# A two-layer hybrid block on one Trainium2 core: the MLP rewritten in two stages over DRAM, with its up-projection in pairs of output tiles by Strassen's seven block products

## The chip, the cores and the metric

The kernel runs on one core of one Trainium2 chip. The metric is the device time of one execution in microseconds (us). The time before is 2850.98 us, the median of three runs (2849.66 to 2864.86). The profile is that of one further execution; its own time stands in the table below, beside its span.

## The reference

Two layers (`DEPTH = 2`) over 1024 tokens of width 1024 (`D`), all in fp32. In each layer a modulated norm, a mixer (differential attention, latent attention and a state-space branch), a residual, a second modulated norm, an MLP of width 4096 (`FF`) and a residual. The part that matters here:

```python
def _sq_relu_mlp(h, w_up, w_down):
    return jnp.square(jax.nn.relu(h @ w_up)) @ w_down

for l in range(DEPTH):
    mod = (cond @ w_ada[l] + b_ada[l])[:, None, :]
    sh_m, sc_m, g_m, sh_f, sc_f, g_f = jnp.split(mod, 6, axis=-1)
    ...
    h = _rmsnorm(x, norm_g[l, 2]) * (1.0 + sc_f) + sh_f
    y = _sq_relu_mlp(h, w_up[l], w_down[l])
    x = x + g_f * _rmsnorm(y, norm_g[l, 3])
```

## The kernel before

Every fp32 operand of a matmul is split in two: a rounded high part, made by a copy on ScalarE (ACT), and the remainder, made by a subtraction on VectorE (DVE). A product of two fp32 blocks is then three matmuls (`mm3`, L192 to L194): high by high, high by low, low by high. Each matmul is 128 x 128 weights against 512 columns, and its sum stands in a PSUM bank (`bank_b` of 512 columns, `bank_s` of 1024, `bank_t` for small things).

The hidden state `hT` (high `hh`, low `hl`) lies transposed in SBUF, 8 blocks `k` of 128 channels by 1024 tokens. `mlp` walks over the 32 tiles `f` of 128 hidden features in groups, `GROUPS = [3]*2 + [2]*11 + [4]`. For each `f`, `load_up` brings 512 KB of `w_up` (L207) and splits it (L210 on ACT, L211 on DVE); `up` makes the two halves of 512 tokens, 24 matmuls each; `Relu` and `Square` on ACT (L221, L222), a product on GpSimd (POOL, L223) and a subtraction on DVE (L224) leave the activated tile `r` split in SBUF; `load_down` brings `w_down` for that `f` and splits it (L229, L232, L233). At the end of a group the eight token tiles each take their down-projection, 6 matmuls for each `f`, into `bank_s`, and the result is added to `y` in SBUF (a copy L273 for the first group, a DVE addition L275 after that). Activations never leave SBUF. Eight slots of the array `split` (`self.R`) hold the weights and the tiles `r`; eight more hold `hT`.

Three streams of other work are threaded through. `late` finishes the residual, norm and transposition of the last token tiles (L1156, L1157, L494, L495, L503 to L506) between the two token halves of the first group. `bg` is the matrix-vector product for the next layer's modulation (`mod_stream`): 56 chunks, each with a 512 KB load (L419), 8 DVE instructions of 128 x 128 (L434) and small matmuls (L445). It is advanced by `next(bg)`, two chunks a call, once for each `f`, and exists in layer 0 alone. `finish` runs the residual and norm of a token tile in the last group.

A scheduler with a timeline of its own orders the instructions of each engine at build time; on the chip each engine then takes them in that order. SP issues all DMAs.

## Time and profile before

| | |
|---|---|
| time, median of 3 runs | 2850.98 us (2849.66 to 2864.86) |
| the profiled execution | 2852.23 us, its span 2850.5 us |
| mean granted TensorE clock | 0.962 |
| instructions | 34146 |
| PE (matmul) busy | 2705.3 us, 95% of the span |
| DVE busy | 1574.3 us, 55% |
| ACT busy | 941.4 us, 33% |
| POOL busy | 595.0 us, 21% |
| DMA moved | 239.66 MB, 84 GB/s over the span |

Busy times are sums over the span and say nothing of where an engine waits. The MLP of layer 0 stands from about 731 to 1451 us, that of layer 1 from about 2141 to 2840 us; the mixers stand before them. PE is TensorE's matmuls, PEld its weight loads, which run beside the matmuls. A matmul's recorded time (0.39 us) is longer than the distance from one to the next (0.23 us), since they are pipelined.

### The profile page before, as it was taken

Reading aid. Unit: us, or ns where it says so; the run is one execution under the profiler, and the core shown is the slowest. Engines: PE = TensorE matmul, PEld = TensorE weight load, DVE = VectorE, ACT = ScalarE, POOL = GpSimd, SP = SyncE. Lnnn points to the kernel's source line nnn. Section 1 sums busy time; section 2 is a strip of 40 time slices with the busy share of each in tenths; the row PEclk is TensorE's granted clock in tenths of the full one; section 3 lists DMA queues with packets and bytes.
Section 4 is the critical chain, followed back from the end, with each engine's and each line's share of the span. In section 5 each row is a group of like instructions: output and inputs, shape, how many; then the busy total and the mean of one; then the engine's idle time right before and its main releaser. Section 6 shows DMA issues by size and latency. Waiting matters only on the chain.

```text
span 2850.5 us, 34146 instructions
## 1 busy us (share of the span) xinstructions
PE 2705.3 (95%) x12914; PEld 2128.9 (75%) x12914; DVE 1574.3 (55%) x2860; ACT 941.4 (33%) x1841; POOL 595.0 (21%) x516
## 2 busy tenths in 40 slices
PE   5799998998899999999979999989989999999998
PEld 4677776676777787887868776667768888888886
DVE  7767677544735557566483667664453344343334
ACT  5243444544421212212243434354443222121122
POOL 1341244201200111111160114241021111110113
PEclk9899999999999999999989999789989999999999
DMA  6441312313322323233340221141142121111112
GB/s 223 115 136 50 93 60 87 109 59 107 115 82 89 96 74 119 80 98 88 101 154 10 64 87 63 54 129 58 49 133 74 45 74 48 41 59 33 57 45 104
DMA packets 258697, 239.66 MB, mean 84 GB/s; under 512 B 22818, under 2 KB 226788, under 8 KB 258532
## 3 DMA queue, kind: packets, MB, share of 16 engines
q1 hardware_dynamic: 258532, 237.47, 26.9%
q8 instruction: 102, 1.67, 0.2%
q14 instruction: 63, 0.52, 0.1%
HBM read 204.56 MB, written 32.87 MB: 83 GB/s over the span
## 4 chain that ended last, share of the span: by engine, by line
PE 74%; DVE 5%; DMA 4%; issue 3%; ACT 2%; POOL 1%; POOLq 0%; SPq 0%; DVEq 0%; ACTq 0%
PE bank_b L192 12%; PE bank_b L194 12%; PE bank_b L193 12%; PE bank_s L192 8%; PE bank_s L193 8%; PE bank_s L194 8%; PE bank_a L737 3%; PE bank_s L790 2%; PE bank_t L750 2%; PE bank_b L1083 1%; DMA arena_f<-in_w_ada 1%; PE bank_s L503 1%; PE bank_a L766 1%; DVE arena_f L434 1%; PE bank_b L884 1%
## 5 line engine op out<-in xcount | busy, mean ns | idle before, releaser
L192 PE MATMUL bank_b<-split 128*128 128x512 f32 (+2 forms) x1952 | 771.5, 396 | 10.1 <-ACT split L505 5.4
L193 PE MATMUL bank_b<-split 128*128 128x512 f32 (+2 forms) x1952 | 755.7, 387 | 4.3 <-DVE split L514 3.6
L194 PE MATMUL bank_b<-split 128*128 128x512 f32 (+2 forms) x1952 | 754.5, 387 | 2.5 <-DVE split L211 2.0
L192 PE MATMUL bank_s<-split 128*128 128x512 f32 (+2 forms) x1152 | 453.5, 396 | 8.3 <-ACT split L1310 3.5
L193 PE MATMUL bank_s<-split 128*128 128x512 f32 (+2 forms) x1152 | 450.7, 391 | 3.3 <-DVE split L1311 1.6
L194 PE MATMUL bank_s<-split 128*128 128x512 f32 (+2 forms) x1152 | 445.5, 390 | 0.7 <-DVE split L224 0.7
L192 PEld LDWEIGHTS bank_b<-split 128*128 128x128 f32 x1952 | 375.7, 193 | 89.2 <-issue 7.6
L193 PEld LDWEIGHTS bank_b<-split 128*128 128x128 f32 x1952 | 375.8, 193 | 74.4 <-issue 4.3
L194 PEld LDWEIGHTS bank_b<-split 128*128 128x128 f32 x1952 | 374.1, 192 | 75.5 <-issue 2.6
L275 DVE TENSOR_TENSOR arena_f<-arena_f,bank_s 128x1024 f32<-128x1024 f32 x208 | 253.1, 1219 | 314.3 <-PE bank_s L194 314.2
L223 POOL TENSOR_TENSOR arena_f<-arena_f 128x512 f32<-128x512 f32 x128 | 164.4, 1284 | 996.0 <-ACT split L222 945.9
L192 PEld LDWEIGHTS bank_s<-split 128*128 128x128 f32 (+1 forms) x1152 | 218.4, 190 | 60.5 <-ACT arena_f L725 4.6
L193 PEld LDWEIGHTS bank_s<-split 128*128 128x128 f32 (+1 forms) x1152 | 219.2, 190 | 50.4 <-issue 2.9
L194 PEld LDWEIGHTS bank_s<-split 128*128 128x128 f32 (+1 forms) x1152 | 219.0, 190 | 45.5 <-DVE split L224 1.4
L221 ACT ACTIVATE arena_f<-bank_b 128x512 f32<-128x512 f32 x128 | 76.1, 595 | 467.2 <-PE bank_b L194 467.1
L725 ACT ACTIVATE arena_f<-bank_s,nm 128x128 f32<-128x128 f32 (+3 forms) x192 | 141.8, 740 | 185.1 <-DVE nm L724 157.2
L724 DVE TENSOR_REDUCE nm<-bank_s 128x1 f32<-128x128 f32 (+3 forms) x192 | 141.7, 751 | 109.3 <-PE bank_s L939 64.7
L232 ACT CAST split<-arena_f 128x1024 fp32r<-128x1024 f32 x64 | 67.3, 1052 | 386.6 <-PE bank_s L194 287.8
L224 DVE TENSOR_TENSOR split<-arena_f,split 128x512 fp32r<-128x512 f32 x128 | 88.3, 690 | 181.1 <-POOL arena_f L223 181.1
L434 DVE SCALAR_TENSOR_TENSOR arena_f<-arena_f,cond 128x128 f32<-128x128 f32 x448 | 154.6, 379 | 60.8 <-DMA arena_f<-in_w_ada 31.0
L233 DVE TENSOR_TENSOR split<-arena_f,split 128x1024 fp32r<-128x1024 f32 x64 | 81.3, 1271 | 84.0 <-ACT split L232 83.9
L790 PE MATMUL bank_s<-split 32*128 32x512 f32 (+3 forms) x576 | 114.7, 376 | 13.2 <-ACT arena_f L725 10.7
(261 smaller groups left out, 3137.2 us busy)
## 6 DMA issues: line engine op xcount, KB each, us to landing
arena_f<-in_w_ada SPq DMA_DIRECT2D x80, 512.0 KB
arena_f<-in_w_down SPq DMA_DIRECT2D x64, 512.0 KB
arena_f<-in_w_up SPq DMA_DIRECT2D x64, 512.0 KB
arena_f<-d_x SPq DMA_DIRECT2D x36, 512.0 KB
d_x<-arena_f SPq DMA_DIRECT2D x24, 512.0 KB
arena_f<-in_w_in SPq DMA_DIRECT2D x20, 512.0 KB
arena_f<-in_w_ada SPq DMA_DIRECT2D x8, 1024.0 KB
arena_f<-in_x SPq DMA_DIRECT2D x16, 512.0 KB
```

Source lines behind the costliest of these rows:

```text
L192: mm(out, wh, xh, start=start, stop=False)
L193: mm(out, wh, xl, start=False, stop=False)
L194: mm(out, wl, xh, start=False, stop=stop)
L223: nc.gpsimd.tensor_mul(t, t, t)
L224: nc.vector.tensor_sub(r[:, 1, sl], t, f32(r[:, 0, sl]))
L233: nc.vector.tensor_sub(wd[:, 1], st, f32(wd[:, 0]))
L275: nc.vector.tensor_add(y[t], y[t], ps)
L434: nc.vector.scalar_tensor_tensor(acc, in0=w[:, k], scalar=self.cond[:, k:k + 1], in1=acc, op0=ALU.mult, op1=ALU.add)
L724: nc.vector.tensor_reduce(nm, S[:, 0:n], axis=AX.X, op=ALU.max, negate=True)
L725: nc.scalar.activation(p[:, 0:n], S[:, 0:n], AF.Exp, bias=nm, accum_out=ls)
L737: nc.tensor.matmul(bk[jj * 64:jj * 64 + 64, 128 * half:256], v[:, 2 * c + jj], e[:, 256:384] if half else e[:, jj * 256:jj * 256 + 256], s ...
L790: nc.tensor.matmul(S[mp][:, c0:c1], Q[rw, a, tok], K[rw, b, c0:c1], start=a == b, stop=a == 1 and c1 < n)
```

## The change

`mlp` becomes two functions. `mlp_up` makes all 32 activated tiles and stores them in a DRAM array `d_r` (4 stores of 256 KB for each pair of tiles). `mlp_down` loads them again, 512 KB for each `f` beside the 512 KB of `w_down`, splits both (ACT and DVE), and makes the down-projection in `GROUPS = [2] + [4]*6 + [2, 4]`.

In `mlp_up` the tiles f = 0 to 3 are made as before, the first two around `late`. The other 28 are made in 14 pairs. A pair's block of the product is 2 x 2 (two feature tiles by two token halves) with the 1024 channels in two halves, and is made of seven products of 12 matmuls each (Winograd's form of Strassen's scheme): 84 matmuls where the plain way has 96. For this four sums of blocks of `hT`, `T[0]` to `T[3]`, are formed once in each layer by `form` (48 instructions of 128 x 512 on DVE, 16 on POOL, and a copy for each on ACT), each pair's weights are combined by four POOL instructions and split in seven `cut`s into a ring of four places, and the seven products are combined by DVE additions that read one operand from PSUM. `bg` is advanced 15 times in `mlp_up` and then once for each `f` in `mlp_down`. In `mlp_down` sixteen slots are taken in turn; for the last two groups their list is sorted, so that these begin again with slot 0.

Around the end of the first stage in layer 1 (tiles f = 0, 1 done, `hT` complete), VectorE's rows before the change, from the last part of `hT` (L506) on, are the subtractions for `r`, `w_up` and `w_down`:

```order
L506 TENSOR_TENSOR split<-bank_s,split 128x8x128
L224 TENSOR_TENSOR split<-arena_f,split 128x512
L233 TENSOR_TENSOR split<-arena_f,split 128x1024
L224 TENSOR_TENSOR split<-arena_f,split 128x512
L211 TENSOR_TENSOR split<-arena_f,split 128x1024
L224 TENSOR_TENSOR split<-arena_f,split 128x512 x2
```

And now, from the last part of `hT` (now L607) to the subtraction for the weights of f = 2 (the first `L200` of 128x1024):

```order
L607 TENSOR_TENSOR split<-bank_s,split 128x8x128 x2
L248 TENSOR_TENSOR arena_f<-split 128x512 x4
L249 TENSOR_TENSOR arena_f<-split 128x512 x4
L250 TENSOR_TENSOR arena_f<-arena_f 128x512 x4
L200 TENSOR_TENSOR split<-arena_f,split 128x512
L248 TENSOR_TENSOR arena_f<-split 128x512
L200 TENSOR_TENSOR split<-arena_f,split 128x512
...
L249 TENSOR_TENSOR arena_f<-split 128x512
L200 TENSOR_TENSOR split<-arena_f,split 128x512
L248 TENSOR_TENSOR arena_f<-split 128x512
L200 TENSOR_TENSOR split<-arena_f,split 128x1024
```

The subtraction that f = 2 needs is now the 22nd VectorE instruction behind `hT` (the 20th in layer 0), behind instructions of `form`. At the same place POOL had its additions of the norm (L495) and the products of `up` (L223):

```order
L495 TENSOR_TENSOR arena_f<-arena_f 128x1024 x7
L223 TENSOR_TENSOR arena_f<-arena_f 128x512
L495 TENSOR_TENSOR arena_f<-arena_f 128x1024
L223 TENSOR_TENSOR arena_f<-arena_f 128x512 x63
L524 TENSOR_TENSOR arena_f<-arena_f 128x1024 x8
```

And has now the whole of form 2, all of it with two inputs from SBUF:

```order
L596 TENSOR_TENSOR arena_f<-arena_f 128x1024 x8
L248 TENSOR_TENSOR arena_f<-split 128x512 x4
L249 TENSOR_TENSOR arena_f<-split 128x512 x3
L250 TENSOR_TENSOR arena_f<-arena_f 128x512 x3
L200 TENSOR_TENSOR split<-arena_f,split 128x512 x3
L249 TENSOR_TENSOR arena_f<-split 128x512
L250 TENSOR_TENSOR arena_f<-arena_f 128x512
L200 TENSOR_TENSOR split<-arena_f,split 128x512
```

So 16 POOL instructions of 128x512 stand ready together with VectorE's. The third place is VectorE in layer 0 before the first down-projections. Before, the work of `bg` (L434) stood in short runs between the subtractions and the additions to `y` (L275):

```order
L434 SCALAR_TENSOR_TENSOR arena_f<-arena_f,cond 128x128 x7
L211 TENSOR_TENSOR split<-arena_f,split 128x1024
L434 SCALAR_TENSOR_TENSOR arena_f<-arena_f,cond 128x128
L224 TENSOR_TENSOR split<-arena_f,split 128x512
L434 SCALAR_TENSOR_TENSOR arena_f<-arena_f,cond 128x128 x3
L224 TENSOR_TENSOR split<-arena_f,split 128x512
```

Now, from the last addition of the last pair (L333) on, long runs of it (now L535) stand ahead of the subtractions (L200) that the second group of the down-projection needs:

```order
L333 TENSOR_TENSOR arena_f<-arena_f,bank_b 128x512
L200 TENSOR_TENSOR split<-arena_f,split 128x1024
...
L535 SCALAR_TENSOR_TENSOR arena_f<-arena_f,cond 128x128 x28
L554 TENSOR_TENSOR arena_f<-bank_t,arena_f 1x128 x2
L535 SCALAR_TENSOR_TENSOR arena_f<-arena_f,cond 128x128 x33
L200 TENSOR_TENSOR split<-arena_f,split 128x1024
L535 SCALAR_TENSOR_TENSOR arena_f<-arena_f,cond 128x128
L200 TENSOR_TENSOR split<-arena_f,split 128x1024
L535 SCALAR_TENSOR_TENSOR arena_f<-arena_f,cond 128x128
L200 TENSOR_TENSOR split<-arena_f,split 128x1024 x3
```

Between L333 and the last of these subtractions stand 74 instructions L535. The mixer of layer 0 keeps its order; in the mixer of layer 1 the scheduler has put the same instructions partly in another order.

The diff, cut to its core:

```diff
-GROUPS = [3] * 2 + [2] * 11 + [4]
+GROUPS = [2] + [4] * 6 + [2, 4]
...
+    def split(self, src, hi, lo, eng=None):
+        self.nc.scalar.copy(hi, src)
+        (eng or self.nc.vector).tensor_sub(lo, src, f32(hi))
...
+    def mlp_up(self, l, hT, bg, late):
...
+        def store(f, hf, t):
+            r = F.get(512) if t.tensor is not self.F.t.tensor else t
+            nc.scalar.activation(r, t, AF.Relu)
+            nc.scalar.activation(r, r, AF.Square)
+            dma(self.d_r[l][f, :, half[hf]], r)
+            F.put(r)
...
+        ws = [load_plain(f) for f in range(2)]
+        for hf in range(2):
+            for f in range(2):
+                up(f, ws[f], hf)
+            self.drain(late)
+        T = [self.slot(2 * n, 2, 4, 512) for n in range(4)]
+        def form(n, a, b, eng):
+            for k in range(4):
+                c, d = F.get(512), F.get(512)
+                eng.tensor_sub(c, f32(a[0][:, k]), f32(b[0][:, k]))
+                eng.tensor_sub(d, f32(a[1][:, k]), f32(b[1][:, k]))
+                eng.tensor_add(c, c, d)
+                self.split(c, T[n][:, 0, k], T[n][:, 1, k], eng)
+                F.put(c, d)
...
+        form(0, B(0, 1), B(0, 0), nc.vector)
+        form(1, B(1, 1), part(0), nc.vector)
+        for f in range(2, 4):
+            w = load_plain(f)
+            for hf in range(2):
+                up(f, w, hf)
+        form(2, B(1, 1), B(0, 1), nc.gpsimd)
+        form(3, B(1, 0), part(1), nc.vector)
+        next(bg, None)
...
+        def forms(i):
+            st = F.get(KD, 2 * P)
+            dma(st, w_up[:, :, i * 2 * P:(i + 1) * 2 * P])
...
+            yield cut(a11)
+            yield cut(a12)
+            s1, s2 = F.get(4, P), F.get(4, P)
+            nc.gpsimd.tensor_add(s1, a21, a22)
+            nc.gpsimd.tensor_sub(s2, s1, a11)
+            yield cut(s2)
+            nc.gpsimd.tensor_sub(a21, a11, a21)
+            yield cut(a21)
+            yield cut(s1)
+            nc.gpsimd.tensor_sub(s2, a12, s2)
+            yield cut(s2)
+            F.put(s1, s2)
+            yield cut(a22)
+            F.put(st)
+        queue = [next(parts) for _ in range(3)]
...
+            for k in range(4):
+                self.mm3(ps, w[0][:, k], w[1][:, k], b[0][:, k], b[1][:, k], k == 0, k == 3)
...
+        for i in range(2, N):
+            f = 2 * i
+            ps, p1 = product(B(0, 0)), F.get(512)
+            nc.scalar.copy(p1, ps)
+            ps, c = product(B(1, 0)), F.get(512)
+            add(c, p1, ps)
+            store(f, 0, c)
...
+            ps = product(part(3))
+            add(u3, u3, ps)
+            store(f + 1, 0, u3)
+            next(bg, None)
...
+    def mlp_down(self, l, y, bg, finish):
+        free = [2, 3, 4, 5, 0, 1, 6, 7, *range(8, 16)]
...
+            if f0 + GROUPS[-1] >= FF // P:
+                free.sort()
...
+            for f in fs:
+                rw.append((load(self.d_r[l][f]), load(w_dn[f * P:(f + 1) * P, :])))
                 next(bg, None)
...
+        self.d_r = [dt(f"d_r{l}", [FF // P, P, T]) for l in range(DEPTH)]
...
+            with self.phase(t=1, b=3):
+                self.mlp_up(l, hT, bg, late)
             with self.phase(t=2, b=2):
-                self.mlp(l, hT, y, bg, late, finish)
+                self.mlp_down(l, y, bg, finish)
```

More of the change, by code (lines that the diff above doesn't have):

```diff
@@ new lines, in mlp_up @@
+        part = lambda n: (T[n][:, 0], T[n][:, 1])
+        form(0, B(0, 1), B(0, 0), nc.vector)
[7 more added lines that the diff above has]
+        next(bg, None)
+        ring = [(hh[:, k, half[1]], hl[:, k, half[1]]) for k in range(4)]
+        ring = [tuple(a.rearrange("p (k f) -> p k f", f=P) for a in r) for r in ring]
@@ new lines, in mlp_up, with product @@
+        N = FF // (2 * P)
+        parts = self.chain(*(forms(i) for i in range(2, N)))
+        queue = [next(parts) for _ in range(3)]
+        def product(b):
+            q = next(parts, None)
+            if q is not None:
+                queue.append(q)
+            w, ps = queue.pop(0), self.bank()
+            for k in range(4):
+                self.mm3(ps, w[0][:, k], w[1][:, k], b[0][:, k], b[1][:, k], k == 0, k == 3)
+            return ps
+        add = nc.vector.tensor_add
+        for i in range(2, N):
[5 more added lines that the diff above has]
+            store(f, 0, c)
+            ps, u2 = product(part(1)), p1
+            add(u2, p1, ps)
+            ps, u3 = product(part(2)), F.get(512)
+            add(u3, u2, ps)
+            ps = product(part(0))
+            add(u2, u2, ps)
+            c = F.get(512)
+            add(c, u3, ps)
+            store(f + 1, 1, c)
+            ps = product(B(1, 1))
+            add(u2, u2, ps)
+            store(f, 1, u2)
+            ps = product(part(3))
+            add(u3, u3, ps)
+            store(f + 1, 0, u3)
+            next(bg, None)
@@ L234, in load_down @@
             F.put(st)
-            return i, wd
+            return i, w
         f0 = 0
```

68 lines of the change are left out of this document (25 added, 43 removed).

## The prediction

> **What bounds the kernel now.** I read first the busy time by stretches of the span (columns: stretch, length, then busy time and count of PE, PEld, DVE, ACT and POOL, the granted clock, the busy share of the DMA engines, GB/s).
>
> ```profile
> core 0: us, PE busy (x) PEld busy (x) DVE busy (x) ACT busy (x) POOL busy (x), PEclk, DMA share, GB/s
> 757.70:1440.00 682.30, 680.32 (x2992) 545.05 (x2991) 383.24 (x699) 145.87 (x213) 95.27 (x115) 1.00 0.31 91
> 1440.00:2141.00 701.00, 656.70 (x3368) 501.31 (x3366) 415.53 (x856) 305.74 (x684) 191.19 (x136) 0.91 0.25 80
> 2161.20:2840.00 678.80, 678.52 (x2992) 561.48 (x2992) 251.61 (x260) 149.31 (x210) 88.38 (x68) 1.00 0.17 53
> ```
>
> The second and fourth rows are the bodies of the two MLPs. There PE is busy without a break at full clock, DVE 56% and 37%, and DMA moves 91 and 53 GB/s. So both are bound by the number of matmuls, and 678.52 / 2992 = 0.2268 us is what one costs. Whatever takes matmuls away gains that; whatever makes PE wait costs its whole length, since there is no slack. Next, the same view around the one long PE idle at the start of the layer 0 MLP, where the last token tiles are still being normed:
>
> ```profile
> 751.00:757.70 6.70, 3.80 (x15) 3.04 (x16) 5.48 (x6) 3.10 (x5) 3.21 (x3) 0.74 0.61 178
> 757.70:765.40 7.70, 7.70 (x28) 6.23 (x27) 2.81 (x8) 0.44 (x1) 0.41 (x2) 0.78 0.43 105
> 765.40:773.10 7.70, 7.70 (x35) 6.37 (x35) 3.14 (x3) 3.92 (x6) 1.63 (x2) 1.00 0.00 0
> ```
>
> After it the clock stays low: 28 matmuls in a stretch that later takes 35, so a long idle costs 7 x 0.2268 = 1.6 us more than itself. Last, for durations, the groups of the helper engines (busy, then mean ns of one) and four rows of the timeline (start, then duration):
>
> ```profile
> L275 DVE TENSOR_TENSOR arena_f<-arena_f,bank_s 128x1024 f32<-128x1024 f32 x208 | 253.1, 1219 | 314.3 <-PE bank_s L194 314.2
> L223 POOL TENSOR_TENSOR arena_f<-arena_f 128x512 f32<-128x512 f32 x128 | 164.4, 1284 | 996.0 <-ACT split L222 945.9
> L221 ACT ACTIVATE arena_f<-bank_b 128x512 f32<-128x512 f32 x128 | 76.1, 595 | 467.2 <-PE bank_b L194 467.1
> L232 ACT CAST split<-arena_f 128x1024 fp32r<-128x1024 f32 x64 | 67.3, 1052 | 386.6 <-PE bank_s L194 287.8
> L224 DVE TENSOR_TENSOR split<-arena_f,split 128x512 fp32r<-128x512 f32 x128 | 88.3, 690 | 181.1 <-POOL arena_f L223 181.1
> L434 DVE SCALAR_TENSOR_TENSOR arena_f<-arena_f,cond 128x128 f32<-128x128 f32 x448 | 154.6, 379 | 60.8 <-DMA arena_f<-in_w_ada 31.0
> L233 DVE TENSOR_TENSOR split<-arena_f,split 128x1024 fp32r<-128x1024 f32 x64 | 81.3, 1271 | 84.0 <-ACT split L232 83.9
> 777.93 1.04 POOL L223 TENSOR_TENSOR arena_f<-arena_f 128x512 f32<-128x512 f32 x1 [4.38 <-ACT split L222]
> 1470.94 2.75 DVE L550 TENSOR_TENSOR split<-arena_f,split 128x512 fp32r<-128x512 f32 x1
> 1473.69 0.67 DVE L550 TENSOR_TENSOR split<-arena_f,split 128x512 fp32r<-128x512 f32 x1
> 1474.28 1.21 DVE L275 TENSOR_TENSOR arena_f<-arena_f,bank_s 128x1024 f32<-128x1024 f32 x1
> ```
>
> The last two rows start 0.59 apart: a DVE instruction on 128x512 costs 0.60, one on 128x1024 1.2, one of L434 154.6 / 448 = 0.345. One on POOL costs 1.04 undisturbed (the row at 777.93).
>
> **The matmuls taken away.** Per layer 14 pairs x 12 = 168 matmuls fewer, 336 in all: 336 x 0.2268 = -76.2 us, all on the path. The down-projection keeps its 1536 a layer. Everything below is what PE waits for anew.
>
> **The sums of `hT`, where POOL and DVE meet.** Form 2 puts 16 POOL instructions with two SBUF inputs beside 48 on DVE. What that does shows at 1467 us, the timeline of both engines:
>
> ```profile
> 1467.07 3.32 POOL L524 TENSOR_TENSOR arena_f<-arena_f 128x1024 f32<-128x1024 f32 x1 [2.48 <-DVE arena_f L523]
> 1470.36 2.78 POOL L495 TENSOR_TENSOR arena_f<-arena_f 128x1024 f32<-128x1024 f32 x1
> 1468.23 2.71 DVE L550 TENSOR_TENSOR split<-arena_f,split 128x512 fp32r<-128x512 f32 x1
> ```
>
> Two DVE subtractions of 0.60 took 2.71 and 2.75 (the second is the row at 1470.94 above) while POOL worked, and the third, alone, 0.67: the engines take turns. For 128x512 on both a turn is 0.60 + 1.04 = 1.64 us. There is a row against it:
>
> ```profile
> 943.97 4.29 DVE L434 SCALAR_TENSOR_TENSOR arena_f<-arena_f,cond 128x128 f32<-128x128 f32 x16 [1.93 <-DMA arena_f<-in_w_ada]
> 946.11 3.06 POOL L223 TENSOR_TENSOR arena_f<-arena_f 128x512 f32<-128x512 f32 x1 [4.78 <-ACT split L222]
> ```
>
> Here 16 short DVE instructions ran at 0.27 each, and POOL's took 3.06 instead of 1.04: DVE kept going and POOL waited. I take turns, because the rows at 1467 are of the kind in `form` (long tensor by tensor instructions), and keep the other as the low end.
> [...]
>
> Now the path. With the rows of the order: the split for f = 2 is DVE's 20th instruction behind `hT` in layer 0, the 22nd in layer 1. PE has then only the second halves of f = 0, 1 left, 48 x 0.2268 = 10.9 us. In full alternation 16 x 1.64 + 3 x 0.60 + 1.2 = 29.2, a stall of 18.3 (layer 1: 19.5); without any, 19 x 0.60 + 1.2 = 12.6, a stall of 1.7 (layer 1: 2.9). Three of POOL's 16 are themselves splits that wait for ACT copies, so some turns fall away: I take 15 and 17. Then f = 2, 3 give PE 96 x 0.2268 = 21.8, to 10.9 + 15 + 21.8 = 47.7. In layer 0 the first pair's first cut stands on DVE behind all 48 instructions of `form`, two splits of 1.2 and 21 of L535: 16 x 1.64 + 32 x 0.60 + 2.4 + 21 x 0.345 = 55.0, a stall of 7. In layer 1 no L535 stands there (47.8) and little is left. Sum 15 + 17 + 7 = +39; bounds 8 and 45.
>
> **The start with two tiles instead of three.** PE's rows at the end of the first halves and where the second begin, layer 0 and then layer 1, with DVE's last part of `hT`:
>
> ```profile
> 747.36 0.39 PE L194 MATMUL bank_b<-split 128*128 128x512 f32 x1
> 757.68 1.06 PE L192 MATMUL bank_b<-split 128*128 128x512 f32 x2
> 741.87 0.60 DVE L434 SCALAR_TENSOR_TENSOR arena_f<-arena_f,cond 128x128 f32<-128x128 f32 x2
> 742.39 1.27 DVE L1156 SCALAR_TENSOR_TENSOR arena_f<-arena_f,rs_y 128x1024 f32<-128x1024 f32 x1
> 2157.34 0.40 PE L194 MATMUL bank_b<-split 128*128 128x512 f32 x1
> 2161.25 0.50 PE L193 MATMUL bank_b<-split 128*128 128x512 f32 x1 [0.54 <-DVE split L506]
> ```
>
> In both PE waits for the norm of the last tokens. Two tiles cover 24 matmuls less, 5.4 us. In layer 0 the first `bg` instructions (16 of L434, the last two at 741.87) stand inside that chain, ahead of L1156; now they come after `hT`, 16 x 0.345 = 5.5 earlier: 0. In layer 1 there are none, and `hT` comes about 1 us earlier for fewer subtractions ahead: +4.5. Bounds 0 and 11.
>
> **The loop of pairs.** PE needs 84 x 0.2268 = 19.05 a pair. DVE has 7 additions and 7 subtractions of 0.60 = 8.4, ACT 7 copies, one more copy and 8 activations, 16 x 0.595 = 9.5, POOL four instructions, 4.2. The additions read PSUM; such a one at L275 is not stretched (mean 1219 against 1.21 alone). The subtractions can be, by up to 4.2 a pair: still 12.6 of 19. In layer 0 `bg` adds 16 x 0.345 = 5.5 a pair on average, to 18.1, and bunches in the first pairs. I take +4 for those, nothing for layer 1; bounds 0 and 30. Stores and loads of the pairs go with the reads of the next: 2 MB in 19 us is 110 GB/s, where the first 50 us moved more than twice that:
>
> ```profile
> 0.00:50.00 50.00, 21.28 (x80) 15.78 (x81) 38.19 (x113) 27.11 (x48) 3.44 (x37) 0.94 0.83 274
> ```
>
> **From up to down, and the second group.** The first groups' loads wait for the last stores only for late tiles; I take +1.5 for both layers (0 to 5). In layer 0, DVE has between the last addition and the last split of the second group 74 L535 and 6 splits, 74 x 0.345 + 6 x 1.22 = 32.8, against the first group's 96 matmuls, 21.8, which start some 2.7 later: 8.3 of stall by the mean duration, 2.8 by the 0.27 of the row at 943.97. No POOL work lies there, so between: +5. In layer 1 none. Reads of 1 MB a tile in 10.9 us are 96 GB/s, hidden; in the first groups of layer 0 with `bg` about 230 to 260, near the most seen, which is one reason not to take less.
>
> **The sorted slots.** For the last two groups slots 0 to 3 come free only with the last matmul of the group before. Then a copy (1.05) for `r`, one for `w_down`, a subtraction (1.13 behind it): 2.1 to 3.3 before PE goes on, twice a layer, 5.5 a layer: +11; bounds 4 and 16.
>
> **Clock.** New long idles in both layers, each with 1.6 behind it: +3 (1 to 5).
>
> **The sum.** -76.2 + 39 + 4.5 + 4 + 1.5 + 5 + 11 + 3 = -8.2. The span becomes 2842.3, and with the 1.7 that the profiled execution took above its span (2852.23 against 2850.5) 2844.0; that execution stands 1.3 above the median shown. The layer 1 mixer is partly reordered; the stretch 1440 to 2141 has 701.00 - 656.70 = 44 us in which PE idles, so I allow 10 either way and put nothing in the sum.
>
> **Rivals.**
> (1) DVE isn't held up by POOL, as at 943.97. `form` then costs 8 instead of 39 and the clock 1 instead of 3: 2844 - 33 = 2811. For it that one row, against it the turns at 1467. Chance 0.22.
> (2) Slower: the loop of pairs doesn't keep PE's pitch. Each weight part goes POOL, ACT, DVE and its subtraction stands on DVE behind an addition that waits for PE; only three products, 8.2 us, lie between. Stretched by turns the chain of two POOL instructions, copy and subtraction is 2 x 1.64 + 0.6 + 1.64 = 5.5, and if an addition that waits for a 2.7 us product falls in, 8.2: no slack. Every 1 us a pair is 28 us. From 0.8 a pair on the kernel is slower by 14; at 1.2 it costs 34 instead of 4: 2874. For it: no row of before has such a chain; against it, the helper engines are half idle. Chance 0.20.
> (3) All stalls hide behind the reordering and the gain stays: -76 + 4.5 + a few, about 2780. Against it: the 22nd place of a split that PE needs after 10.9. Chance 0.08.
> That the matmuls are not saved isn't a rival: PE's order holds 84 a pair.
>
> **How the numbers follow.** The likeliest is the sum, chance 0.50, by its own bounds 2824 to 2864. No measurement of this kernel tells less than 0.5%, 14.3 us, from no change. Of the likeliest's 0.50 I put 0.16 faster (stalls at the lower bounds), 0.29 same, 0.05 slower; rival 1 is 0.21 faster, 0.01 same; rival 2 0.15 slower, 0.05 same; rival 3 0.08 faster. Sum: faster 0.45, same 0.35, slower 0.20. The range, 2804 to 2874, takes in rival 1 and rival 2 up to its price; outside stand rival 3 and the dearer half of rival 2, 0.18.
>
> **What the profile will show.** Right if PE idles some 15 us before f = 2 in both layers, DVE and POOL there alternating at 1.6; if a pair's PE time is 19; if the idle before the second group in layer 0 and before the last two groups has L200 as releaser. Wrong by rival 1 if DVE's L248 last 0.6 there while POOL's last 2 and more; by rival 2 if within the pairs PE waits regularly for L200 or L199.

## The result, and the profile after

| | before | after |
|---|---|---|
| median of 12 runs on one chip | 2851.95 us (2843.69 to 2864.86) | 2867.91 us (2863.39 to 2885.04) |
| the profiled execution | 2852.23 us, its span 2850.5 | 2878.17 us, its span 2876.5 |
| mean granted clock | 0.962 | 0.946 |
| PE busy | 2705.3 us, 95% | 2661.0 us, 93% |
| DVE, ACT, POOL busy | 55, 33, 21% | 61, 38, 23% |
| DMA moved | 239.66 MB | 306.80 MB |

The changed kernel is slower by half a per cent: ratio 1.0054, interval [1.0035, 1.0073]. 2844 was predicted, 0.2% faster. A second run of it (`after2`, below) gave 1.0043 [1.0023, 1.0063]; the two intervals overlap. The profiled execution of after lies 10 us above its median, so the accounts below, made between the two profiles, explain 26 us where the medians differ by 16.

I split each span at the last part of `hT` and at the last matmul of the down-projection. The stretches between are the whole MLPs of layer 0 and 1 behind `hT`. Busy time by these stretches, of before (columns as in the prediction's first fence):

```profile
756.60:1467.10 710.50, 708.52 (x3122) 568.39 (x3121) 405.41 (x747) 162.03 (x249) 115.11 (x122) 1.00 0.31 95
2161.20:2839.60 678.40, 678.35 (x2992) 561.48 (x2992) 251.42 (x259) 149.31 (x210) 87.98 (x68) 1.00 0.17 52
```

The same of after, and then the layer 0 MLP cut at the first product of the pairs, at their last addition and behind the first group of the down-projection, and the layer 1 MLP at the first two of these and ahead of its last two groups:

```profile
757.80:1502.40 744.60, 697.07 (x2982) 549.07 (x2983) 500.42 (x915) 242.69 (x382) 142.79 (x133) 0.96 0.44 140
2186.30:2864.90 678.60, 659.61 (x2855) 541.88 (x2854) 347.40 (x409) 233.19 (x347) 134.91 (x79) 0.98 0.31 107
757.80:821.20 63.40, 45.03 (x158) 35.24 (x159) 56.12 (x78) 20.63 (x36) 41.66 (x26) 0.78 0.30 92
821.20:1114.30 293.10, 285.30 (x1233) 222.76 (x1232) 214.59 (x431) 133.47 (x230) 74.13 (x74) 0.99 0.51 160
1114.30:1165.00 50.70, 34.27 (x126) 23.39 (x126) 38.65 (x112) 19.39 (x25) 2.39 (x12) 0.80 0.64 194
2186.30:2240.80 54.50, 43.26 (x158) 33.76 (x158) 45.37 (x54) 20.19 (x36) 38.77 (x20) 0.82 0.16 50
2240.80:2506.60 265.80, 265.80 (x1174) 220.11 (x1173) 145.03 (x200) 137.96 (x223) 81.35 (x53) 1.00 0.38 128
2792.90:2864.90 72.00, 67.68 (x287) 54.18 (x285) 43.86 (x60) 17.77 (x29) 14.78 (x7) 0.98 0.33 117
```

Read length minus PE's busy time. Before, PE idles 2.0 and 0.05 us in the two MLPs; after, 47.5 and 19.0. The saving is there all the same: PE has 140 and 137 records fewer, and 24 matmuls a layer more stand behind `hT` than before, the tile that no longer stands ahead of it. In layer 1 saving and losses cancel (678.4 and 678.6); in layer 0 the MLP is 34.1 longer. With `hT` 1.2 later, the mixer of layer 1 (from the end of one MLP to the next `hT`) 683.9 instead of 694.1 and the tail 0.7 longer, that is 1.2 + 34.1 - 10.2 + 0.2 + 0.7 = 26.0 us, the difference of the spans.

Where PE idles in layer 0: 18.4 between `hT` and the first product (63.40 - 45.03), 16.4 at the start of the down-projection, 7.8 in the pairs, 4.9 in what is left. In layer 1: 11.2 before the first product, nothing in the pairs, 3.4 at the start of the down-projection (for a PSUM bank that ACT's copy L373 empties), 4.3 in the last two groups. The granted clock is the second sign: 0.78, 0.80 and 0.82 in just the three stretches with the longest idles. The spells at half clock, and beside them one at full clock (same view of after, cut where the clock changes):

```profile
775.90:786.10 10.20, 7.88 (x18) 5.77 (x19) 10.20 (x16) 6.42 (x12) 8.56 (x1) 0.50 0.08 27
786.10:803.00 16.90, 16.90 (x76) 13.97 (x75) 9.86 (x18) 4.49 (x9) 8.87 (x10) 1.00 0.61 181
806.60:820.30 13.70, 5.42 (x13) 4.24 (x14) 13.46 (x22) 3.64 (x7) 8.89 (x6) 0.50 0.34 101
1147.90:1165.00 17.10, 7.91 (x17) 4.61 (x18) 14.77 (x34) 6.63 (x8) 0.20 (x1) 0.50 1.09 323
```

At half clock (0.50) 18 matmuls fill 7.88 us, nearly twice their price (18 x 0.2268 = 4.08). At that clock half of PE's busy time in all such spells is lost: 17.4 us in the layer 0 MLP (2.2 before) and 10.6 in layer 1 (0 before).

What PE waits for. First the sums of `hT`: the timeline of after (start, duration, then the instruction, and in brackets the idle time ahead of it with its releaser) on ACT, PE, DVE and POOL:

```profile
772.10 0.62 ACT L199 CAST split<-arena_f 128x512 fp32r<-128x512 f32 x1 [15.58 <-DVE arena_f L250]
775.99 0.79 PE L192 MATMUL bank_b<-split 128*128 128x512 f32 x1 [5.40 <-ACT split L199]
780.29 0.80 PE L194 MATMUL bank_b<-split 128*128 128x512 f32 x1 [2.23 <-DVE split L200]
757.69 5.86 DVE L248 TENSOR_TENSOR arena_f<-split 128x512 f32<-128x512 f32 x4
763.47 6.86 DVE L249 TENSOR_TENSOR arena_f<-split 128x512 f32<-128x512 f32 x4
770.26 4.63 DVE L250 TENSOR_TENSOR arena_f<-arena_f 128x512 f32<-128x512 f32 x4
756.66 6.34 POOL L248 TENSOR_TENSOR arena_f<-split 128x512 f32<-128x512 f32 x4 [3.22 <-ACT split L606]
777.53 12.90 POOL L200 TENSOR_TENSOR split<-arena_f,split 128x512 fp32r<-128x512 f32 x3 [4.40 <-ACT split L199]
```

Twelve DVE instructions took 17.35 us, 1.45 each instead of 0.60: nine of them stand 1.69 apart, the turns of the prediction (1.64 there), and the last two 0.60. POOL then waits 4.40 for a copy, and when it comes back DVE is in a run of its own. The first of POOL's three takes 10.41 (in the row 775.90:786.10 above it is all that POOL does) and ends 1.16 after the end of DVE's run at 786.79; the other two, with DVE idle, take 1.28 each. So both of the prediction's rows describe one stretch, one after the other.

PE's wait for f = 2 is 5.40 + 2.23 in layer 0 (6.80 + 2.88 in layer 1), where 15 and 17 were expected. Only the 2.23 is for the DVE split that the prediction had followed. The 5.40 is for ACT's copy of the same weights: in ACT's queue it stands behind the first copies of the sums, and for the first of these ACT idles 15.58 us until DVE has made its L250 in turns with POOL.

Next the 10.72 us ahead of the first product, on SP, ACT and PE:

```profile
751.59 26.74 SPq L218 DMA_DIRECT2D d_r<-arena_f  x2
800.38 0.40 SPq L273 DMA_DIRECT2D arena_f<-in_w_up  x1
808.42 0.38 SPq L273 DMA_DIRECT2D arena_f<-in_w_up  x1
814.21 1.14 ACT L199 CAST split<-arena_f 128x512 fp32r<-128x512 f32 x2 [5.95 <-DMA arena_f<-in_w_up]
814.88 0.80 PE L192 MATMUL bank_b<-split 128*128 128x512 f32 x1 [10.72 <-ACT split L199]
```

The wait of about the predicted length has another cause: not DVE's queue, but the load of the first pair's weights. SP spends 26.74 us on two stores to `d_r` whose activations aren't made yet, with no other issue in its rows for that time, then issues loads of the modulation, and comes to the two loads of `w_up` in these rows only at 800.38 and 808.42. By the semaphores of the trace ACT's copy at 814.21 waits for the second of them: it lands at 814.19 (the first had landed at 807.71), and SP issued it when a store to `d_r`, itself issued at 805.07, had landed at 808.40.

The last is the start of the down-projection in layer 0:

```profile
1144.60 0.35 SPq L345 DMA_DIRECT2D arena_f<-d_r  x1
1140.00 8.72 DVE L535 SCALAR_TENSOR_TENSOR arena_f<-arena_f,cond 128x128 f32<-128x128 f32 x30 [0.52 <-DMA arena_f<-in_b_ada]
1125.60 1.04 ACT L199 CAST split<-arena_f 128x1024 fp32r<-128x1024 f32 x1 [5.47 <-DMA arena_f<-d_r]
1159.70 1.04 ACT L199 CAST split<-arena_f 128x1024 fp32r<-128x1024 f32 x1 [3.62 <-DMA arena_f<-in_w_down]
1152.85 1.22 PE L192 MATMUL bank_s<-split 128*128 128x512 f32 x2 [5.08 <-ACT split L199]
1160.79 1.22 PE L192 MATMUL bank_s<-split 128*128 128x512 f32 x2 [4.20 <-ACT split L199]
```

The predicted L535 run is there (30 in 8.72 us), but ACT's copies wait for the loads of `r` and `w_down` themselves, at 194 GB/s in this stretch, with a DMA share of 1.09 in its last third. SP issues the load of `r` above only at 1144.60, behind a store of the modulation's result (`d_mod`) that had waited 6.4 us for DVE's L554, which stands behind another run of L535. So DVE's queue does hold PE up here, by way of SP. Of the 16.4 us 9.3 are waits for ACT's copies L199, 3.7 for the copies L373 and 1.6 for a small matmul of the modulation.

### The profile page after: what moved, and what is told of

Its sections match the earlier page's. It is cut to its first block, busy times and chain, and to the rows that moved or that the text cites. A ratio compares the mean times of both kernels' runs of the same rounds, so it can differ in the third digit from the quotient of the medians.

```text
span 2876.5 us, 34698 instructions
## 1 busy us (share of the span) xinstructions
PE 2661.0 (93%) x12578; PEld 2078.7 (72%) x12578; DVE 1747.1 (61%) x3148; ACT 1098.4 (38%) x2105; POOL 665.7 (23%) x532
## 2 busy tenths in 40 slices
DMA packets 257231, 306.80 MB, mean 107 GB/s; under 512 B 25442, under 2 KB 200740, under 8 KB 257060
## 5 line engine op out<-in xcount | busy, mean ns | idle before, releaser
L192 PE MATMUL bank_b<-split 128*128 128x512 f32 (+2 forms) x1840 | 736.1, 400 | 44.1 <-ACT split L199 24.1
L194 PE MATMUL bank_b<-split 128*128 128x512 f32 (+2 forms) x1840 | 716.6, 390 | 7.5 <-DVE split L200 6.5
L193 PE MATMUL bank_b<-split 128*128 128x512 f32 (+2 forms) x1840 | 718.2, 390 | 0.4 <-DVE split L651 0.3
L199 ACT CAST split<-arena_f 128x512 fp32r<-128x512 f32 (+1 forms) x364 | 274.3, 778 | 748.5 <-PE bank_s L193 360.0
L192 PE MATMUL bank_s<-split 128*128 128x512 f32 (+2 forms) x1152 | 455.6, 399 | 29.2 <-ACT split L199 12.6
L192 PEld LDWEIGHTS bank_b<-split 128*128 128x128 f32 x1840 | 358.1, 195 | 125.3 <-ACT split L199 25.8
L194 PEld LDWEIGHTS bank_b<-split 128*128 128x128 f32 x1840 | 356.5, 194 | 79.6 <-DVE split L200 9.3
L193 PEld LDWEIGHTS bank_b<-split 128*128 128x128 f32 x1840 | 358.4, 195 | 68.1 <-issue 4.5
L200 DVE TENSOR_TENSOR split<-arena_f,split 128x512 fp32r<-128x512 f32 (+1 forms) x356 | 334.9, 956 | 111.7 <-ACT split L199 111.5
L375 DVE TENSOR_TENSOR arena_f<-arena_f,bank_s 128x1024 f32<-128x1024 f32 x128 | 155.9, 1218 | 269.8 <-PE bank_s L194 269.8
L826 ACT ACTIVATE arena_f<-bank_s,nm 128x128 f32<-128x128 f32 (+4 forms) x192 | 141.9, 741 | 189.3 <-DVE nm L825 163.9
L535 DVE SCALAR_TENSOR_TENSOR arena_f<-arena_f,cond 128x128 f32<-128x128 f32 x448 | 163.9, 394 | 65.4 <-DMA arena_f<-in_w_ada 28.7
L625 POOL TENSOR_TENSOR arena_f<-arena_f 128x1024 f32<-128x1024 f32 x16 | 43.7, 2731 | 596.9 <-DVE arena_f L624 593.8
L854 ACT COPY arena_f<-bank_t 128x512 f32<-128x512 f32 (+1 forms) x160 | 86.7, 542 | 104.9 <-PE bank_t L851 94.5
L838 PE MATMUL bank_a<-arena_f 128*64 128x256 f32 (+1 forms) x640 | 108.4, 398 | 13.6 <-ACT arena_f L854 12.1
```

The costliest lines, as they stand in the source:

```text
L192: mm(out, wh, xh, start=start, stop=False)
L193: mm(out, wh, xl, start=False, stop=False)
L194: mm(out, wl, xh, start=False, stop=stop)
L199: self.nc.scalar.copy(hi, src)
L200: (eng or self.nc.vector).tensor_sub(lo, src, f32(hi))
L375: nc.vector.tensor_add(y[t], y[t], ps)
```

## The experiments

The theory: the products bring what was counted, and a few new waits take it back: the sums on POOL, the first pair's late load, the crowded start of the down-projection, the sorted slots, each with low clock behind it. The rivals: the staging over DRAM costs as much by itself whatever the products do; or low clock alone, and not the waits, makes the difference. "MLP 0", "MLP 1" and "mixer 1" in this table are the stretches of the profiles as above; ratios are against runs of before on the same chip in the same series, whose median lies between 2852 and 2859.

| kernel | median us | ratio | MLP 0 | mixer 1 | MLP 1 |
|---|---|---|---|---|---|
| before | 2851.95 | 1 | 710.5 | 694.1 | 678.4 |
| after | 2867.91 | 1.0054 [1.0035, 1.0073] | 744.6 | 683.9 | 678.6 |
| after2 | 2868.79 | 1.0043 [1.0023, 1.0063] | 746.5 | 680.2 | 675.6 |
| dveform | 2853.98 | 0.9991 [0.9972, 1.0009] | 735.3 | 686.3 | 667.7 |
| slots | 2859.67 | 1.0024 [0.9991, 1.0057] | 744.1 | 669.3 | 668.8 |
| bgtok | 2860.11 | 1.0012 [0.9987, 1.0038] | 735.7 | 679.4 | 682.3 |
| firstload | 2860.45 | 1.0025 [0.9998, 1.0052] | 735.0 | 683.0 | 677.0 |
| fill | 2871.14 | 1.0058 [1.0029, 1.0086] | 742.6 | 679.9 | 676.3 |
| plain2 | 2909.34 | 1.0187 [1.0147, 1.0226] | 734.0 | 700.4 | 695.2 |
| plainfix | 2887.80 | 1.0093 [1.0066, 1.0119] | 719.5 | 706.1 | 688.9 |
| best2 | 2802.91 | 0.9813 [0.9781, 0.9846] | 697.7 | 679.0 | 656.9 |
| best3 | 2809.99 | 0.9840 [0.9808, 0.9873] | 702.2 | 674.0 | 660.2 |
| best4 | 2814.54 | 0.9857 [0.9828, 0.9886] | 704.8 | 684.4 | 655.2 |

**The sums all on DVE (`dveform`).**

```diff
-        form(2, B(1, 1), B(0, 1), nc.gpsimd)
+        form(2, B(1, 1), B(0, 1), nc.vector)
```

> Form 2 is made by DVE instead of POOL, nothing else. Theory (turns on the shared path of DVE and POOL hold up the split for f = 2, and the idle that follows drops the clock): the split for f = 2 is DVE's 20th instruction behind hT, now undisturbed at 0.60 each, so it lands 12.6 us after hT instead of 22.5 (layer 0) and 23.8 (layer 1). PE's idle before f = 2 falls from 8 and 10 us to about 2 each, the clock loss behind it by some 8 in all: about 2868 - 22 = 2846. Rival (DVE's own work is the limit, POOL takes load off it): DVE's 64 instructions take 38 us instead of 29, the first cut comes 10 us later in both layers: 2868 + 15 = 2883.

Its ratio to before is 0.9991. The stretch from `hT` to the first product in layer 0 and 1, and DVE's rows:

```profile
750.60:806.80 56.20, 42.61 (x160) 33.93 (x160) 53.10 (x85) 20.65 (x36) 13.92 (x11) 0.80 0.33 103
2172.20:2215.60 43.40, 39.81 (x159) 32.02 (x160) 43.18 (x66) 20.97 (x36) 4.70 (x3) 0.92 0.26 85
750.56 4.90 DVE L248 TENSOR_TENSOR arena_f<-split 128x512 f32<-128x512 f32 x8
762.00 1.22 DVE L200 TENSOR_TENSOR split<-arena_f,split 128x1024 fp32r<-128x1024 f32 x1
796.25 0.79 PE L192 MATMUL bank_b<-split 128*128 128x512 f32 x1 [10.73 <-ACT split L199]
```

Without POOL beside it DVE makes eight in 4.90, 0.6 each, and the split for f = 2 is done 12.6 us behind `hT` although more instructions are DVE's. PE's wait for f = 2 is gone, and the MLPs are 9.3 and 10.9 shorter. Two engines were slower at this (1.45 us an instruction on DVE in after) than one of them. The edit has a second effect, which this run can't part from the first: ACT now makes the copy for f = 2 at 758.36, ahead of the copies of the sums. The wait for the first product stays, 10.73 where it was 10.72: it isn't made by the turns.

**The slots of the last groups (`slots`).** The group of two ahead of the last goes on in turn; only the last group takes slots 0 to 7, in their first order.

```diff
-            if f0 + GROUPS[-1] >= FF // P:
-                free.sort()
+            if last:
+                free = [i for i in [2, 3, 4, 5, 0, 1, 6, 7] if i in free]
```

> The list of free slots is not sorted for the group before the last, which then takes slots freed a group earlier; the last group takes 2, 3, 4, 5, 0, 1, 6, 7 in this order, so that only its third and fourth tile wait for the group before. Theory (the idle before the last two groups is the wait for slots): 5.7 us of PE idle in layer 0 and 5.0 in layer 1 go to about 2 each, and up to 3 of low clock: 2868 - 9 = 2859. Rival (the wait is for the loads of the tiles from DRAM): 2868.

The start of the last groups in layer 1, after and then this kernel:

```profile
2792.90:2822.00 29.10, 24.78 (x103) 19.16 (x101) 20.55 (x18) 7.66 (x8) 0.00 (x0) 0.97 0.18 57
```
```profile
2771.00:2800.00 29.00, 27.66 (x119) 21.75 (x118) 17.02 (x15) 3.90 (x4) 0.00 (x0) 1.00 0.15 50
```

Idle there falls from 4.3 to 1.3: the wait is where the prediction put it, and this order takes most of it away. The layer 1 MLP is 9.8 shorter, of which 3.0 lie here; the rest is less idle and low clock in stretches that the edit doesn't touch. In layer 0 the idle at the same place falls from 4.9 to 1.3 as well, yet its MLP stays (744.1). The interval of the whole holds both 1 and after's ratio, so its gain in time isn't settled by this run.

**The modulation's work behind the loads (`bgtok`).** In `mlp_down` the two advances a group move from the loop of loads into the loop of token tiles. The last line resets the record by which the arena chooses its places.

```diff
             for f in fs:
                 rw.append((load(self.d_r[l][f]), load(w_dn[f * P:(f + 1) * P, :])))
-                next(bg, None)
...
+                if t in (1, 4) and not last:
+                    next(bg, None)
...
+        F.stamp = [0] * len(F.stamp)
```

> In the down-projection the modulation work of the next layer is advanced between the token tiles (two calls a group) instead of once for each load. The memory's age marks are reset at the end of the MLP so that the build finds room; the layer 1 mixer may be laid out otherwise. Theory (PE waits in its order for that work's small matmuls and for splits that stand behind its runs on DVE): between 1114 and 1165 us some 20 us of PE idle and 6 of low clock go to a few: 2868 - 20 = 2848. Rival (DMA, at over 200 GB/s there, is the limit): 2868, with PE waiting for loads at the same place.

The first 50.7 us behind the last addition in layer 0, to set against after's 1114.30:1165.00:

```profile
1108.50:1159.20 50.70, 43.33 (x180) 32.27 (x179) 39.21 (x82) 23.07 (x27) 1.44 (x7) 0.93 0.67 216
```

PE does 180 matmuls in it instead of 126; idle falls from 16.4 to 7.4, the clock rises from 0.80 to 0.93, and the layer 0 MLP loses 8.9 us. The DMA share is no lower (0.67 and 0.64). So it was the order of the work, not the amount of the loads. The edit moves the modulation's loads, stores and DVE work together, so that it was SP's queue is read from the trace of after and not from this run. What idle is left is for ACT's copies to `y`, in whose queue copies wait for loads of `r`. The layer 1 MLP is 3.7 longer, and the whole took 2860 where 2848 was expected.

**The first pair's load ahead (`firstload`).**

```diff
+        first = F.get(KD, 2 * P)
+        dma(first, w_up[:, :, 4 * P:6 * P])
         for f in range(2, 4):
...
-            st = F.get(KD, 2 * P)
-            dma(st, w_up[:, :, i * 2 * P:(i + 1) * 2 * P])
+            st = first
+            if i > 2:
+                st = F.get(KD, 2 * P)
+                dma(st, w_up[:, :, i * 2 * P:(i + 1) * 2 * P])
```

> The 1 MB of weights of the first pair gets its buffer and is issued before the tiles f = 2, 3 instead of behind their stores; nothing else. Theory (the 10.9 us of idle before the first product in layer 0 wait for that load, issued at 808 us behind stores and modulation loads on SP): the idle falls to 3 or less and the low clock behind it (13.7 us at half speed, from 806.6) mostly goes: -12 in layer 0, 2868 - 12 = 2856. Rival (as the prediction had it: the first cut stands on DVE behind all of the sums of hT and the modulation work): no change in that idle, 2868.

```profile
744.72 0.38 SPq L258 DMA_DIRECT2D arena_f<-in_w_up  x1
772.38 0.79 PE L194 MATMUL bank_b<-split 128*128 128x512 f32 x1 [7.40 <-DVE split L200]
750.00:804.30 54.30, 43.53 (x159) 33.69 (x159) 54.30 (x64) 20.38 (x35) 33.69 (x24) 0.83 0.22 69
```

The load now goes at 744.72, 5 us ahead of `hT`, where the load that after waits for went 51 us behind it, and the first product waits 2.40 instead of 10.72. The wait for the sums shows at f = 2 as 7.40, and the stretch falls from 63.4 to 54.3. That shows the cause; in layer 1, where no modulation loads stand in the way, the stretch stays (54.5 and 54.8).

**Low clock filled up (`fill`).** Matmuls whose result nobody reads: 30 ahead of f = 2, and in layer 0 44 behind f = 3.

```diff
+        def warm(n):
+            ps = self.bank("t")
+            for k in range(n):
+                nc.tensor.matmul(ps, hh[:, k % 8, 0:P], hh[:, k % 8, half[0]], start=k == 0, stop=k == n - 1)
...
+            if f == 2:
+                warm(30)
...
+        if l == 0:
+            warm(44)
```

> The changed kernel with 74 extra matmuls in layer 0 and 30 in layer 1, whose results nobody uses, on TensorE around the end of the norm of the last tokens and the first matmul of f = 2 (in layer 0 some also stand between f = 3 and the first pair, and the scheduler mixes them a little among the others). 30 of them are 6.8 us, about the idle they stand in. Theory (the low clock behind f = 2 comes from the idle ahead of it): the idle before f = 2 turns into work, the clock stays at full speed there, and the low-clock loss of the first 57 us of layer 0 (6.7 us of it) and of the first 48 of layer 1 (6.1) goes to 2 or less: some 8 to 10 less in those stretches, if the fillers themselves aren't late. Rival (the clock falls for another reason, as it did at 980 us without a long idle): the low-clock rows stay, and the fillers cost what they don't hide, 0 to +5.

```profile
753.40:818.80 65.40, 51.62 (x206) 39.76 (x205) 63.98 (x92) 20.64 (x35) 38.29 (x29) 0.90 0.31 97
2175.90:2229.40 53.50, 42.25 (x170) 33.10 (x171) 49.04 (x53) 20.18 (x35) 42.88 (x21) 0.94 0.20 64
```

The clock rises from 0.78 to 0.90 and from 0.82 to 0.94 ((1 - 0.78) x 63.40 / 0.5 = 27.9 us at half clock become 13.1, and 19.6 become 6.4). The stretches keep their length, 65.4 and 53.5 where after has 63.4 and 54.5 and 8 to 10 us less were expected, and the ratio is after's. The idle in them is 13.8 and 11.3 where after has 18.4 and 11.2, so in layer 1 the clock rose with as much idle; which idle brings the low clock this run doesn't show. What the low clock is worth by itself this run doesn't settle, since the extra matmuls weren't free: all 30 in layer 1 and 38 of the 74 in layer 0 ran ahead of `hT`, and the stretches hold 48 and 12 matmuls more than after's (206 for 158, 170 for 158), 10.9 and 2.7 us at full clock. That low clock alone is the cause is refuted by the accounts above: the idle in the two MLPs is 64.5 us more than before, the loss at half clock 25.8 more.

**The staging without the products (`plain2`, `plainfix`).** All pairs are made as f = 0 to 3 are, 24 matmuls a half, with the staging kept. `plain2` resets the arena's record as `bgtok` does; `plainfix` has the new slots and the token calls of `bgtok` instead. In both the weights take eight slots in turn.

```diff
-        for f in range(2, 4):
+        for f in range(2, FF // P):
             w = load_plain(f)
             for hf in range(2):
                 up(f, w, hf)
+            if f % 2:
+                next(bg, None)
```

> The two stages over DRAM alone: all 32 tiles are made by 24 matmuls for each half as before the change, stored, and loaded again; no block products, no sums of hT (with the same reset of age marks). 336 matmuls more than in the changed kernel, 76 us. Theory (some half of the loss belongs to the sums of hT and the late weights of the first pair, the rest to the second stage: the waits for the modulation work, the slots, the shorter cover at the start and the low clock behind them): the staging costs 35 to 45 against the kernel before: 2852 + 40 = 2892. Rival (the traffic through DRAM and its copies are the whole loss of 76 + 16 = 92): 2944.

> The two stages with the plain up-projection (24 matmuls for each half of all 32 tiles), with the mended slots and the modulation work between the token tiles, as in best2. Beside best2 it lacks the seven products and the sums of hT only. Theory (once their waits are hidden, the products bring nearly all of their 336 matmuls): 2803 + 76 less some 5 for what is left of the sums = about 2874. Rival (the staging mended costs what it cost before, 53 over the kernel before, less the 18 that slots and modulation work brought in the changed kernel): 2890.

`plain2`, the two MLPs, and then `plainfix`:

```profile
762.40:1496.40 734.00, 720.33 (x3148) 573.48 (x3147) 342.10 (x672) 194.79 (x280) 32.20 (x58) 0.99 0.43 135
2196.80:2892.00 695.20, 690.71 (x3022) 569.68 (x3021) 194.27 (x186) 178.26 (x241) 14.74 (x7) 0.99 0.30 100
```
```profile
765.60:1485.10 719.50, 718.16 (x3146) 570.61 (x3145) 344.17 (x669) 193.98 (x281) 33.20 (x58) 1.00 0.44 138
2191.20:2880.10 688.90, 687.32 (x3023) 567.34 (x3021) 195.24 (x187) 178.00 (x241) 14.79 (x7) 1.00 0.30 100
```

The staging alone costs 1.87%, 53 us, of which 40 lie in the MLPs; after is some 40 us better than it. So the products bring gain and the staging does not. With its waits mended (`plainfix` idles 1.3 and 1.6) the staging still costs 9.0 and 10.5 in the MLPs, of which 24 matmuls a layer that now stand behind `hT` are 5.4. The rival that staging costs as much whatever the products do is half true: it does cost, but in the MLPs these edits bring the 40 down to 19.5. The whole is 2887.80, near the 2890 that the rival had.

**All mended together (`best2`).** `dveform`, `firstload`, the new slots and the token calls of `bgtok`; beside that the weights of f = 2 and 3 are loaded and split with those of f = 0 and 1, ahead of everything and in slots of their own, and `form(3, ...)` stands behind the cuts of the first pair:

```diff
-        ws = [load_plain(f) for f in range(2)]
+        ws = [load_plain(f) for f in range(4)]
+        first = F.get(KD, 2 * P)
+        dma(first, w_up[:, :, 4 * P:6 * P])
...
-            w = load_plain(f)
             for hf in range(2):
-                up(f, w, hf)
+                up(f, ws[f], hf)
-        form(2, B(1, 1), B(0, 1), nc.gpsimd)
-        form(3, B(1, 0), part(1), nc.vector)
-        next(bg, None)
+        form(2, B(1, 1), B(0, 1), nc.vector)
...
         queue = [next(parts) for _ in range(3)]
+        form(3, B(1, 0), part(1), nc.vector)
```

> All mended at once: the weights of f = 0 to 3 loaded and split before the last tokens are normed (own slots each), the first pair's weights loaded at the same place, all sums of hT on DVE with the last of them behind the first cuts, modulation work between the token tiles in the down-projection, and the unsorted slots. Theory (what was lost is PE idle in these five places and the low clock behind them): the MLP of layer 0 falls from 747 us by 30 to 40, that of layer 1 from 681 by 20 to 25: 2868 - 58 = 2810, faster than the kernel before by 1.5%. Rival (waits move on: the loop of pairs in layer 0 with the modulation work, or the transition to the second stage, takes up what is freed): 2845.

Its MLPs, and its stretches from `hT` to the first product:

```profile
755.30:1453.00 697.70, 686.73 (x2984) 541.37 (x2983) 501.71 (x928) 240.83 (x383) 125.60 (x118) 0.99 0.46 148
2132.00:2788.90 656.90, 652.27 (x2855) 537.63 (x2853) 346.83 (x422) 231.35 (x345) 112.49 (x63) 0.99 0.32 109
755.30:793.40 38.10, 37.74 (x162) 30.76 (x161) 37.87 (x60) 15.79 (x30) 13.05 (x5) 0.97 0.25 83
2132.00:2175.60 43.60, 40.35 (x162) 32.64 (x161) 39.49 (x63) 16.12 (x30) 17.30 (x4) 0.91 0.12 41
```

0.9813 [0.9781, 0.9846], 52 us under before and some 65 under after. Of the 50.4 us between the spans of before and of this profile 34.3 lie in the two MLPs; 15.1 lie in the layer 1 mixer, which no edit touches and which differs by more than that between the variants. The stretch to the first product is 38.1 and 43.6 (after has 63.4 and 54.5); as many matmuls back to back would take about 37. Idle in the MLPs is 11.0 and 4.6 instead of 47.5 and 19.0. Against `plainfix`, the same staging with the plain products, its MLPs are 1408.4 - 1354.6 = 53.8 us shorter, of the 76.2 that the matmuls are worth.

**Cover moved back (`best3`, `best4`).** `best2` with the first token halves of three or four tiles ahead of the last tokens, instead of two.

```diff
-            for f in range(2):
+            for f in range(3 if hf == 0 else 2):
                 up(f, ws[f], hf)
```

> best2 with the first token halves of three tiles instead of two ahead of the norm of the last tokens, as many as the kernel before had. Theory (the cover given up at the start cost PE idle: 5.97 + 1.10 us ahead of hT in layer 0 of best2, 3.6 in layer 1): 24 matmuls, 5.4 us, move into that idle, and the low clock behind it shrinks: 2803 - 9 = 2794. After hT 120 matmuls (27.2 us) are left to hide the first three sums of hT, which take DVE 28.9: about even. Rival (the scheduler's order of the norm moves back by as much as the matmuls take): 2803.

> The same with four tiles ahead. Theory: all of the idle ahead of hT is covered (-11 and its low clock), but behind hT only 96 matmuls, 21.8 us, are left to hide 28.9 us of sums on DVE: 7 or more of new idle before the first product in each layer: about 2803 again. Rival (the sums aren't the limit there, since the first cut does not depend on them): 2787.

0.9840 and 0.9857: no gain over `best2`. The stretch ahead of `hT` isn't what is left to win here; what more PE has there it waits for later, behind `hT`, where waits of up to 4.7 us for splits and 4.5 for additions appear. Expected were 2794 and about 2803.

**After once more (`after2`).** The kernel unchanged.

> The changed kernel again, unchanged, for a second profile. The first had a span of 2876.5 where the median time is 2868. Theory (what differs between executions lies in the mixers, where the clock falls at other places): the MLP of layer 0 takes 747 +- 4 again, that of layer 1 681 +- 4, and the rest is 10 shorter. Rival (the MLP with its waits is what varies): one of the MLPs is 10 shorter.

Its MLPs repeat within 3.0 us (746.5 and 675.6), so the account by stretches stands for the kernel and not for one execution; the layer 1 mixer is 3.7 off. The 10 us less outside the MLPs that were expected didn't come: it was 0.9. Over all variants that mixer, of which none changes a line, runs from 669 to 706 us. Differences of a few us between whole kernels are therefore no proof for a step; that is why the stretches are compared.

## Why the prediction was wrong, by its own steps

The sum came to -8.2 and the spans differ by +26.0; the MLPs with `hT` and the tail alone by +36.2. What failed, by size: low clock, where +3 stood and 22.8 more was lost; the start of the down-projection, where +6.5 stood and PE idled 19.8; the start of the MLPs, where +4.5 stood and it cost 12. The sums of `hT` cost less idle than the 39 that stood, 29.6, and by another path. Term by term:

- **Matmuls, -76.2: right.** 168 a layer less the 24 that moved behind `hT` is 144, and the records, of which a few can be missing, show 140 and 137; 53.8 us of it is shown as time by `best2` against `plainfix`.
- **The sums of `hT`, +39: the wait is there, the size and one mechanism are off.** PE idles 18.4 and 11.2 us between `hT` and the first product, where 22 and 17 stood. For f = 2 it was 7.6 and 9.7 instead of 15 and 17: turns at first, as taken, then DVE kept going, as in rival 1's row. Most of it, 5.4 and 6.8, came through ACT's queue, which the prediction had left out. The 7 for the first cut became 10.72 for a reason that the prediction had not named: the order of SP's queue. `dveform` left that wait as it was and `firstload` took it away.
- **Low clock, +3: the step that failed most.** Half clock took 17.4 + 10.6 - 2.2 = 25.8 us of PE's busy time. The 1.6 for each idle came from a single row after a 3 us idle, and two were priced. The traces have eleven spells of half clock in the two MLPs, where before has one, and they lose 1.3 to 4.2 us each: the long ones are 10 to 17 us, with a further wait in them (the 2.23 in that of 10.2) or much of the wait itself (8.3 of the 10.72 in that of 13.7). What of it could be had back alone `fill` leaves open; with waits gone the clock of the same stretch rises from 0.82 to 0.92 in `dveform` (layer 1; in layer 0, where a wait of 10.73 stays, from 0.78 to 0.80), from 0.80 to 0.93 in `bgtok`, and from 0.78 and 0.82 to 0.97 and 0.91 in `best2`.
- **The start with two tiles, +4.5: layer 0 wrongly at nothing.** `hT` was to come 5.5 earlier and came 1.2 later, so the 5.4 of cover were paid in full, 6.6 together. The 1.2 is less than `hT` differs between the two profiles of the same kernel (757.8 and 760.6), but the 5.5 earlier didn't come. The work of the modulation is gone from the chain, but a wait for POOL is in it. Timeline of DVE and POOL in after:

```profile
738.19 2.34 DVE L1255 TENSOR_TENSOR fs<-fss 128x1 f32<-128x1 f32 x1
744.88 1.29 DVE L1257 SCALAR_TENSOR_TENSOR arena_f<-arena_f,rs_y 128x1024 f32<-128x1024 f32 x1
737.28 3.24 POOL L596 TENSOR_TENSOR arena_f<-arena_f 128x1024 f32<-128x1024 f32 x1 [1.23 <-PE bank_s L604]
```

  An addition of one column takes 2.34 us (its counterpart L1154 took 0.15) and ends at 740.53, when POOL's L596 ends at 740.52; L1257 starts 2.5 later than its counterpart L1156 did at 742.39. In layer 1 the 5.4 of cover were paid as well, 12 in all.
- **The loop of pairs, +4: right for layer 1, short for layer 0.** 14 pairs took 265.8, 19.0 each, without a gap: rival 2 is refuted there. (That rival's own sum is off: 0.8 a pair, 22.4 where 4 stood, gives 2862, 11 above before and not 14.) Layer 0 took 293.1 with 7.8 of idle; most of the rest is the modulation's own small matmuls, which before had as well. One of the gaps is a queue: DVE waits 6.57 us for a load of `w_ada`, behind it stands the addition that frees PE's bank, and PE idles 3.54.

```profile
977.39 0.71 DVE L535 SCALAR_TENSOR_TENSOR arena_f<-arena_f,cond 128x128 f32<-128x128 f32 x1 [6.57 <-DMA arena_f<-in_w_ada]
981.50 0.77 PE L192 MATMUL bank_b<-split 128*128 128x512 f32 x1 [3.54 <-DVE arena_f L327]
```

- **From up to down and the second group, +6.5: too small.** 16.4 in layer 0, for the most part from loads that SP issues behind the modulation's loads and stores, and 3.4 in layer 1. The prediction had estimated 230 to 260 GB/s for these groups and priced only the splits in DVE's queue. `bgtok` shows that the order of the modulation's work is the cause: 7.4.
- **The sorted slots, +11: right in place, near in size.** 4.9 and 4.3 in the last stretches.
- **The layer 1 mixer, nothing, 10 either way:** -10.2 in the profiles.

Put together against the sum: idle in both MLPs 45.5 + 19.0 where 60.5 stood, +4.0; low clock +22.8; the start in both layers +7.5; tail +0.7; the mixer -10.2; what is left, +9.4, was not traced to rows (the modulation's small matmuls, which now come mostly in twos and not in fours, are a guess). That makes 34.2, the gap between -8.2 and 26.0. The total of PE's idle was nearly right by luck: smaller at the sums, larger at two loads. Of rival 1 half came true (DVE keeps going, later), of rival 3 nothing.

One thing stays open: the medians differ by 16, ten less than the profiles. Both profiled executions of after lie above their medians, by 10.3 and 7.4. The longer executions have the lower granted clock (0.954 at 2863.39 us, 0.944 at 2885.04); where in the span it falls no run here shows.

## What to carry to other kernels

Fewer matmuls pay only where PE stays fed at the seams: here 76 us of saving was lost at the joints of two stages, and six small edits of order and place brought some 65 us back. At each joint follow the first load of the next stage through the queue that issues it, in order, past every store that waits for a result; a wait on a compute engine's queue is only one of the candidates. Then follow the copies that stand ahead of the one that is needed, on every engine that makes a part of the operand. Work shared out to a second engine slowed both here (128x512 on DVE from 0.60 to 1.45 us, one on POOL from 1.28 to 10.41): price it by a row where both run, and try the faster one alone.
